# The output projection of an encoder layer as seven block products in one written order

## The chip, the cores and the metric

The kernel is one launch on one core of a Trainium2 chip. The metric is the device time of that launch in microseconds (us); the time of a version is the median of its runs. A profile of one execution is read beside it. In it PE is the matrix engine (TensorE), PEld its loading of stationary operands, DVE is VectorE, ACT ScalarE, POOL GpSimd, and SP the engine whose queue issues most DMAs.

## The reference

One encoder layer is applied to two inputs, 1024 rows ("sample") and 256 rows ("prompt") of width 1024, with the same weights. Two attention branches give `o_a` and `o_b`; a gate merges them, the merged rows go through the output projection, and a squared-ReLU MLP follows.

```python
merged = gates[:, :, 0] * (o_a.reshape(b, S, A_Q) @ w_branch_a) + gates[:, :, 1] * (o_b @ w_branch_b)
x = x + merged @ w_out                      # the output projection: 1280 x 1024 times 1024 x 1024
h = _rmsnorm(x, g_mlp)
return x + jnp.square(jax.nn.relu(h @ w_up)) @ w_down
```

All of it is float32. The kernel keeps that precision by splitting every matmul operand into a high part (a copy rounded to the matrix engine's fast float32 form, on ACT) and a low part (the operand minus the high part, on DVE), and by adding three matmuls, low x high, high x low and high x high, for each product.

## The kernel before

The 1280 rows are 10 tiles of 128 rows (`NT`), tiles 0 to 7 the sample, 8 and 9 the prompt. The stages follow one another on the matrix engine: input projection and attention, the two branch products with their gates, the output projection, then the MLP's up and down products.

**The branch products** are 48 jobs in the list `jobs`. Each makes 128 columns of `merged`, transposed, for one of three row blocks (`BLOCKS`: rows 0-511, 512-1023, 1024-1279) and puts them into the wide tile `mT`. The last 12 jobs are the second half of the `a` columns, block by block. During them `fetch` and `prepare` load and split the projection's weights.

**The output projection** (from L1605) runs in two halves `hh` of 512 output columns. In each, for each row tile `t`, `split_m` splits the tile's eight 128 x 128 pieces of `mT`, `mm3` (L192) makes 24 matmuls 128 x 128 by 128 x 512 (8 pieces, three matmuls each) in one PSUM bank, and DVE adds the bank to the residual tile `x2[t]` (L1653, L1662). In the second half the tile is then normalised: ACT squares it and sums (L1665), ACT takes the root (L1667), DVE the reciprocal (L1672), DVE scales it with `gm` into `xn[t]` (L1673), SP stores `x2[t]`. One tile later PE turns `xn` with eight transposes (`turned`, L336) into two banks of tag `pt`, of which there are two, and ACT copies these out (L1577, L1560).

**The MLP's up product** is already made of seven block products in place of eight (the scheme of Strassen and Winograd). Its left operands are the four quarters of the normalised sample rows and three sums of them, `S1`, `S2`, `S3` (and later `S4`), made on DVE by `combine` (L1587, L1589, L1592), first for 3/4 of the columns, then for the last quarter. `halves` splits them (L310 high part on ACT, L312 low part on DVE). The product on the quarter `A11` comes first, then `A12`, `S2`, `S3`, `S1`, `A22`. A product is `seven` (L345): 12 matmuls. `right_pair` makes the matching sums of the weights (L391) and splits them.

**What sets the order.** Until the projection's second half, a planner orders each engine's instructions and gives out buffers. From `tc.manual_schedule` on, which stands at the start of the second half, each engine executes its instructions in the order in which the code writes them: an instruction that waits holds up all that follow on its engine. So the places of `next(turning)`, `next(more)`, `part(t + 2)` and `steps_of(sums, ..)` in the loop over `t` are the queue orders of ACT and DVE. The buffers are 33 slots of 4 KB per partition with tag `m` (`slot`), 10 of tag `w` (`wslot`), 6 in the pool `late` (tag `l4`), and eight PSUM banks: `mm` 3, `sc` 2, `pt` 2, `pv` 1.

Of the kernel before, what the change touches and what calls it, by code (L numbers as in the profile page):

```python
# [10 lines left out]
F32 = mybir.dt.float32  # L11
# [4 lines left out]
P = 128  # L16
D = 1024
# [80 lines left out]
def encoder_kernel(  # L98
# [8 lines left out]
    def x_rows(t):  # L107
        return x_sample[0, P * t : P * (t + 1), :] if t < 8 else x_prompt[0, P * (t - 8) : P * (t - 7), :]
# [18 lines left out]
    def slot(name, shape=(P, D), dt=F32):  # L127
        return slots.tile(list(shape), dt, name=name, tag="m", bufs=N_M)
# [4 lines left out]
    def qslot(name, shape, dt=F32):  # L133
        return narrows[0].tile(list(shape), dt, name=name, tag="q", bufs=N_Q)
# [49 lines left out]
    def split(hi, lo, src):  # L184
        nc.scalar.activation(hi, src, AF.Copy)  # L185
        nc.vector.tensor_tensor(lo, src, hi.bitcast(F32), op=ALU.subtract)  # L186
# [25 lines left out]
    n_out = len(specs)  # L212
    for h in range(2):
        for i in range(4):
            specs.append((w_out3[:, 2 * i : 2 * i + 2, 512 * h : 512 * h + 512], (P, 2, 512), wslot))
    specs[n_out + 2] = specs[n_out + 2][:2] + (slot,)
# [92 lines left out]
    def split_steps(hi, lo, src):  # L309
        nc.scalar.activation(hi, src, AF.Copy)  # L310
        yield
        nc.vector.tensor_tensor(lo, src, hi.bitcast(F32), op=ALU.subtract)  # L312
        yield
# [54 lines left out]
    def right_pair(cols, out, make=wslot, vector=False, step=KC):  # L368
# [13 lines left out]
        def part(src, shape):  # L382
            out.append((wslot("whi", shape, F32R), wslot("wlo", shape, F32R)))
            yield from split_steps(*out[-1], src)
# [973 lines left out]
    def split_m(t, hh, out):  # L1358

        n = 2 if hh else KC  # L1360
        mhi = [qslot("mhi", (P, n, P), F32R) if hh else slot("mhi", (P, n, P), F32R) for _ in range(KC // n)]
        mlo = slot("mlo", (P, KC, P), F32R)
        for c in range(0, KC, 2):
            split(mhi[c // n][:, c % n : c % n + 2, :], mlo[:, c : c + 2, :], mT.at(c, P * t, P, 2))
            yield
        out += [(mhi[k // n][:, k % n, :], mlo[:, k, :]) for k in range(KC)]

    first_m = []
    early_m = split_m(0, 0, first_m)
    if True:  # L1370
# [100 lines left out]
        sgs = {}  # L1471

# [38 lines left out]
        for i, (x, b, c) in enumerate(jobs):  # L1511
# [7 lines left out]
            if i in (1, 4, 22, 26):  # L1519
                fetch()  # L1520
            elif i in (5, 8, 33, 35):
                w_as[(5, 8, 33, 35).index(i)] = weight(0)
            elif i in (38, 40, 42, 44):
                prepare()
# [14 lines left out]
            if i > len(jobs) - 6:  # L1539
                next(early_m, None)  # L1540

    att_pool.close()


    x2 = [slot(f"x2_{t}") for t in range(NT)]
    for t in range(NT):
        nc.sync.dma_start(x2[t], x_rows(t))
# [60 lines left out]
    with ExitStack() as pre:  # L1608
        late = pre.enter_context(tc.tile_pool(name="late", bufs=4))

        def lslot(name, shape=(P, D), dt=F32):
            return late.tile(list(shape), dt, name=name, tag="l4", bufs=6)

        for i in (4, 5, 6):
            specs[n_out + i] = specs[n_out + i][:2] + (lslot,)
        gm = slot("gm2")
        nc.sync.dma_start(gm, g_mlp[0].partition_broadcast(P))
        xn = {}
        p0 = []
        b0 = right_up(0, p0, slot)  # L1620

        def ahead():

            yield from b0
            yield from halves(A11, raws_h[0, 0])
            yield from halves(A12, raws_h[0, 1])

        more, sums = ahead(), combine()
        for hh in range(2):
            sl = slice(512 * hh, 512 * hh + 512)  # L1630
            ws = [weight(0) for _ in range(4)]
            parts = {}
            if hh:

                ctx.enter_context(tc.manual_schedule(engines=ALL))

            def part(t):
                if t < NT:
                    parts[t] = []
                    run(split_m(t, hh, parts[t]))  # L1640

            if hh:
                part(0)
            else:
                parts[0] = first_m
            part(1)
            for t in range(NT):
                m = parts.pop(t)
                ps = bank("mm")
                run(mm3(ps, [(m[k], (ws[k // 2][0][:, k % 2, :], ws[k // 2][1][:, k % 2, :]))  # L1650
                             for k in range(KC)]))
                if hh == 0:
                    nc.vector.tensor_tensor(x2[t][:, sl], x2[t][:, sl], ps, op=ALU.add)  # L1653
                    part(t + 2)
                    if 2 <= t < 6:
                        prepare()
                    elif t in (6, 7):
                        next(more)
                    continue
                turning = (turn_sample if t < 9 else turn_prompt)(t - 1) if t else iter(())  # L1660
                next(turning, None)
                nc.vector.tensor_tensor(x2[t][:, sl], x2[t][:, sl], ps, op=ALU.add)  # L1662
                xn[t] = slot("xn", (P, D))
                ss = small.tile([P, 1], F32, name="ss")
                nc.scalar.activation(xn[t], x2[t], AF.Square, accum_out=ss)  # L1665
                sd = small.tile([P, 1], F32, name="sd")
                nc.scalar.activation(sd, ss, AF.Sqrt, bias=eps, scale=1.0 / D)  # L1667
                if 0 < t < 7:
                    next(more)
                steps_of(sums, (0, 1, 4)[max(t - 7, 0)])  # L1670
                rs = small.tile([P, 1], F32, name="rs")
                nc.vector.reciprocal(rs, sd)  # L1672
                nc.vector.scalar_tensor_tensor(xn[t], x2[t], rs, gm, op0=ALU.mult, op1=ALU.mult)  # L1673
                nc.sync.dma_start(scr_x[t], x2[t])
                next(turning, None)
                part(t + 2)
                steps_of(more, (1, 1, 1, 1, 1, 3, 2, 0, 0, 0)[t])
                steps_of(sums, (2, 3)[t - 7] if 6 < t < 9 else 0)
        run(sums)
        run(halves(S2, combined[S2]))  # L1680
    narrow.close()
# [6 lines left out]
    C11, C12, C21, C22 = range(4)  # L1688

# [206 lines left out]
    with ExitStack() as pre:  # L1896
# [30 lines left out]
        def up(j, b, parts, hooks):  # L1927
# [7 lines left out]
            start = begin(parts)  # L1935
# [107 lines left out]
```

## Time and profile before

| | us |
|---|---|
| median of 3 runs | 1674.67 |
| lowest and highest run | 1673.53, 1675.32 |
| the profiled execution, first to last instruction (its span) | 1672.7 |
| first matmul of the output projection | 769.2 |
| its last matmul's start | 885.0 |
| matmuls of the output projection | 480 |

The profile's own time for the execution is its span; what lies before the first and after the last instruction is not in it. The median of the runs is 1.97 us above the span. The page gives the busy time of each engine, the span in 40 slices, the chain of work that ended last (followed back from the last instruction through what released each step), and groups of instructions with count and mean duration. The trace answers for any stretch: the instructions of one engine in order of time, the same chain in detail, or busy time by stretch.

### The profile page before, as it was taken

The page shows a single profiled execution, that of the slowest core. Times are in us where ns is not written, and L with a number is a line of the kernel's source. Part 1 is how long each engine was busy: PE and PEld are TensorE (multiplying, and loading weights), DVE is VectorE, ACT ScalarE, POOL GpSimd, SP SyncE. Part 2 cuts the span into 40 slices and gives each one's busy share as a digit, 9 for nine tenths or more (in the row PEclk, how much of TensorE's full clock was granted, in tenths as well). Part 3 has the DMA queues.
Part 4 walks back from the last instruction along what each step waited for, and adds up shares of the span by engine and source line. Part 5 has one row for each costly group of instructions (what it writes and reads, how often), then busy time and mean ns, then how long its engine had stood idle before and what let it go on. Part 6 is the DMA issues. An engine that isn't in the chain of part 4 may idle for free.

```text
span 1672.7 us, 24767 instructions
## 1 busy us (share of the span) xinstructions
PE 1661.8 (99%) x9256; PEld 1413.9 (85%) x9256; DVE 951.1 (57%) x1534; ACT 714.3 (43%) x1473; POOL 494.3 (30%) x372
## 2 busy tenths in 40 slices
PE   9999999999999999999999999999999999999998
PEld 7898888888888888888888888888888888888886
DVE  6732233455654565667278545445456775867665
ACT  6232323345654655654176333333334333333435
POOL 1212222111112352100100656455554250514240
PEclk9999999999999999999999999999999999999999
DMA  7416552666667794845121443343356934733333
GB/s 256 150 54 126 134 132 75 165 196 189 198 184 228 192 236 134 284 135 193 38 89 59 161 160 120 121 161 125 116 191 230 362 113 137 253 104 107 120 120 126
DMA packets 224176, 262.45 MB, mean 157 GB/s; under 512 B 29486, under 2 KB 153694, under 8 KB 224056
## 3 DMA queue, kind: packets, MB, share of 16 engines
q1 hardware_dynamic: 217000, 242.69, 45.4%
q0 software_dynamic: 6720, 17.65, 5.1%
q8 instruction: 73, 1.20, 0.3%
q10 hardware_dynamic: 336, 0.53, 0.1%
q14 instruction: 47, 0.39, 0.1%
HBM read 175.13 MB, written 90.92 MB: 159 GB/s over the span
## 4 chain that ended last, share of the span: by engine, by line
PE 96%; ACT 2%; DVE 1%; DMA 1%; issue 0%; SPq 0%; DVEq 0%; ACTq 0%
PE dn L345 22%; PE x L345 19%; PE mm L192 14%; PE z L345 10%; PE v L819 6%; PE y L345 5%; PE mm L345 5%; PE pv L345 3%; PE sc L345 3%; PE pt L1193 2%; PE pv L1209 2%; PE sc L553 1%; PE pv L600 1%; PE pt L586 1%; PE tr L336 1%; PE sc L1167 1%
## 5 line engine op out<-in xcount | busy, mean ns | idle before, releaser
L345 PE MATMUL dn<-dhi,ulo 128*128 128x512 f32 x448 | 174.3, 389 | 0.0
L345 PE MATMUL dn<-dlo,uhi 128*128 128x512 f32 x448 | 174.3, 389 | 0.0
L345 PE MATMUL dn<-dhi,uhi 128*128 128x512 f32 x448 | 174.3, 389 | 0.0
L345 PE MATMUL x<-chi,wlo 128*128 128x512 f32 x424 | 166.5, 393 | 0.0
L345 PE MATMUL x<-clo,whi 128*128 128x512 f32 x424 | 165.6, 390 | 0.0
L345 PE MATMUL x<-chi,whi 128*128 128x512 f32 x424 | 165.0, 389 | 0.0
L312 DVE TENSOR_TENSOR wlo<-ta,whi 128x1024 fp32r<-128x1024 f32 x30 | 56.3, 1876 | 174.0 <-ACT whi L310 174.0
L312 DVE TENSOR_TENSOR wlo<-raw,whi 128x1024 fp32r<-128x1024 f32 x60 | 89.6, 1494 | 103.1 <-ACT whi L310 98.2
L391 POOL TENSOR_TENSOR tb<-raw 128x512 f32<-128x512 f32 x25 | 32.3, 1290 | 363.7 <-DMA raw<-in_w_in_dram 111.8
L345 PEld LDWEIGHTS dn<-dhi,ulo 128*128 128x128 f32 x448 | 84.1, 188 | 17.6
L345 PEld LDWEIGHTS dn<-dhi,uhi 128*128 128x128 f32 x448 | 84.1, 188 | 17.4
L345 PEld LDWEIGHTS dn<-dlo,uhi 128*128 128x128 f32 x448 | 84.1, 188 | 17.4
L345 PEld LDWEIGHTS x<-chi,whi 128*128 128x128 f32 x424 | 79.6, 188 | 17.1
L345 PEld LDWEIGHTS x<-chi,wlo 128*128 128x128 f32 x424 | 79.8, 188 | 15.1
L345 PEld LDWEIGHTS x<-clo,whi 128*128 128x128 f32 x424 | 79.8, 188 | 14.6
L1735 POOL TENSOR_TENSOR t<-raw,t 128x1024 f32<-128x1024 f32 x16 | 46.4, 2924 | 149.2 <-DMA raw<-in_w_down_dram 149.2
L186 DVE TENSOR_TENSOR ulo<-uraw,uhi 128x1024 fp32r<-128x1024 f32 x56 | 86.1, 1558 | 4.4 <-ACT uhi L185 4.4
L1886 DVE TENSOR_TENSOR v<-v,dn 128x512 f32<-128x512 f32 x90 | 59.7, 683 | 42.3 <-PE dn L345 42.3
L186 DVE TENSOR_TENSOR dlo<-raw,dhi 128x1024 fp32r<-128x1024 f32 x32 | 50.1, 1590 | 46.3 <-ACT dhi L185 45.3
L1986 POOL TENSOR_TENSOR u<-u,u 128x640 f32<-128x640 f32 x16 | 25.1, 1569 | 173.3 <-ACT u L1904 173.3
L345 PE MATMUL dn<-dhi,up 128*128 128x512 f32 x224 | 73.5, 389 | 0.0
L345 PE MATMUL z<-chi,wlo 128*128 128x512 f32 x184 | 71.6, 389 | 0.0
(319 smaller groups left out, 4619.2 us busy)
## 6 DMA issues: line engine op xcount, KB each, us to landing
scr_u<-u SPq DMA_DIRECT2D x112, 320.0 KB, 2.6
uraw<-scr_u SPq DMA_DIRECT2D x56, 512.0 KB, 3.9
raw<-in_w_down_dram SPq DMA_DIRECT2D x36, 512.0 KB, 6.7
raw<-in_w_up_dram SPq DMA_DIRECT2D x32, 512.0 KB, 5.2
raw<-in_w_in_dram SPq DMA_DIRECT2D x25, 512.0 KB, 5.2
sg<-scr_g SPq DMA_DIRECT2D x32, 256.0 KB, 6.2
uraw<-scr_u SPq DMA_DIRECT2D x28, 256.0 KB, 4.5
qk<-scr_kb SPq DMA_DIRECT2D x48, 128.0 KB, 2.6
```

The source lines that it names most:

```text
L186: nc.vector.tensor_tensor(lo, src, hi.bitcast(F32), op=ALU.subtract)
L192: nc.tensor.matmul(ps, a, b, start=i == 0, stop=i == len(seq) - 1)
L312: nc.vector.tensor_tensor(lo, src, hi.bitcast(F32), op=ALU.subtract)
L336: nc.tensor.transpose(ps[:, P * i : P * (i + 1)], xn[t][:, P * k : P * (k + 1)], ident)
L345: nc.tensor.matmul(ps, a, b, start=first and i == 0, stop=last and i == len(seq) - 1, skip_group_check=True)
L391: (nc.vector if vector else nc.gpsimd).tensor_tensor(o, x, y, op=ALU.subtract)
L819: nc.tensor.matmul(ps[:, :n], a, b, start=k == 0 and j == 0, stop=k == KC - 1 and j == 2)
L1193: nc.tensor.transpose(ps[:, P * k : P * k + P], s[:, h, P * b : P * b + P], ident)
L1209: nc.tensor.matmul(pv[HALVES[h], P * i : P * i + P], src, pt[:, at + 2 * b + h, :], start=b == 0, stop=b == W // P - 1, skip_group_check=True)
L1735: nc.gpsimd.tensor_tensor(o, a, b, op=ALU.subtract)
L1886: nc.vector.tensor_tensor(v, v, ps, op=ALU.add)
L1986: nc.gpsimd.tensor_tensor(u[S1], u21, u22, op=ALU.add)
```

## The change

The projection's left operand (1024 sample rows and 256 prompt rows, seen as two halves of 640 rows) and `w_out` are cut into four blocks each, and seven products of 640 x 512 by 512 x 512 take the place of eight. Each product `n` has five steps `t` (four tiles of 128 rows of the sample half and one of the prompt), a step being `six`: 12 matmuls 128 x 128 by 128 x 512. Results that several blocks of the output share stay in their PSUM bank: products 1 and 2 are joined in one bank, and so are 3, 4, 5 and 6, and after each product DVE adds what the bank holds then to the residual (`total`), 35 additions of 128 x 512 in place of 20.

The sums of the left operands (`sum1` to `sum4`) and of the weight blocks (`differ`) are on GpSimd. So are the low parts of the weights of products 5 and 6 and of the up product's first weights (`low`). The blocks of `w_out` are loaded eight times in all, 1 MB each, in two DMAs. The manual order begins before the first product. The rows of the first half are finished in product 4 and normalised there, those of the second half in product 6; a row's `scale` comes one step after its `norm`, and its transposes two steps after. The sums for the up product start in the last step (34), after the copies of tile 6. Tile 7 is turned, and the rest of the sums made and `S2` split, in the middle of the up product's first block (`entered`).

```diff
-    def split(hi, lo, src):
+    def split(hi, lo, src, low=None):
         nc.scalar.activation(hi, src, AF.Copy)
-        nc.vector.tensor_tensor(lo, src, hi.bitcast(F32), op=ALU.subtract)
+        (low or nc.vector).tensor_tensor(lo, src, hi.bitcast(F32), op=ALU.subtract)
...
+        ORDER = (A12, S1, S4, A11, S2, S3, A22)
+        TO = (C11, C22, C12, C11, C12, C22, C21)
+        TAGS = (("mm", "mm", "mm", "sc", "sc"), ("pt", "pt", "pv", "sc", "sc"), None, ("mm", "mm", "mm", "sc", "sc"),
+                None, None, None)
...
+        def differ(self, o, a, b):
+            for x, y, z in zip(self.b[o], self.b[a], self.b[b]):
+                nc.gpsimd.tensor_tensor(x, y, z, op=ALU.subtract)
...
+        def right(self, n, name, low=None):
+            out = self.rights[n] = []
+            for src in self.b[name]:
+                hi, lo = wslot("whi", (P, 2, 512), F32R), wslot("wlo", (P, 2, 512), F32R)
+                split(hi, lo, src, low)
...
+        def left(self, n, i):
...
+            split(hi, lo, self.source(n, i))
...
+        def sum1(self, i):
...
+            nc.gpsimd.tensor_tensor(self.s1[i], self.quarter(1, 0, i), self.quarter(1, 1, i), op=ALU.add)
...
+        def product(self, n, t):
...
+            six(self.banks[t], self.rights[n], lefts, n in (0, 1, 3), n in (0, 2, 6))
+
+        def total(self, n, t):
+            c = self.TO[n]
+            v = x2[self.row(c, t)][:, 512 * (c % 2) : 512 * (c % 2) + 512]
+            nc.vector.tensor_tensor(v, v, self.banks[t], op=ALU.add)
+
+        def ahead(self, n):
+
+            if n == 0:
+                self.right(1, "t")
+                self.block("b22", 1, 1)
+                self.rows(1)
+                yield
+                for i in range(3):
+                    self.left(1, i)
+                    self.sum2(i)
+                    yield
+                for i in range(3):
+                    self.sum4(i)
...
+            elif n == 2:
+                self.right(3, "b11")
+                self.block("b22", 1, 1)
+                yield
+                for i in range(3):
+                    self.left(3, i)
+                    self.sum3(i)
+                    yield
...
+            elif n == 4:
+                self.right(5, "b22", nc.gpsimd)
+                self.block("b21", 1, 0)
+                yield
+                for i in range(3):
+                    self.left(5, i)
+                    yield
+                self.differ("b21", "b21", "t")
+            elif n == 5:
+                self.right(6, "b21", nc.gpsimd)
+                yield
+                for i in range(3):
+                    self.left(6, i)
+                    yield
...
     def right_up(j, out, make=wslot):
-        return right_pair([w_up3[:, :, c : c + P] for c in (2 * P * j, 2 * P * j + P)], out, make, j == 1)
...
+        return right_pair([w_up3[:, :, c : c + P] for c in (2 * P * j, 2 * P * j + P)], out, make, j == 1,
+                          low=None if j else nc.gpsimd)
...
+    for n in range(7):
+        side = out.ahead(n)
...
+        for t in range(5):
+            step = 5 * n + t
+            out.product(n, t)
+            turning = iter(())
+            if turns and turns[0][0] <= step:
+                r = turns.pop(0)[1]
+                turning = (turn_sample if r < 8 else turn_prompt)(r)
+            next(turning, None)
+            out.total(n, t)
+            if scales:
+                scale(scales.pop())
+            if n in (4, 6):
+                r = out.row(0 if n == 4 else 2, t)
+                scales.append(r)
+                turns.append((step + 2, r))
+                norm(r)
+            next(turning, None)
+            next(side, None)
+            if step == 28:
+                steps_of(b0, 2)
+            if 29 <= step <= 32:
+                steps_of(lefts, 2)
+            if step in (30, 31, 33):
+                steps_of(b0, 2)
+            if step == 34:
+                steps_of(sums, 6)
+    scale(scales.pop())
+    run(b0)
+    pre.close()
+
+    def entered():
+        run(turn_sample(7))
         run(sums)
         run(halves(S2, combined[S2]))
...
-        def begin(parts):
+        def begin(parts, mid=None):
 
             x, y = bank("mm", "x"), bank("pt", "y")
-            seven(x, A11, parts[0], 0, last=False)
+            seven(x, A11, parts[0], 0, last=False, mid=mid)
```

In the code after the change, `norm` is the squaring and the root on ACT, `scale` the reciprocal and the scaling on DVE with the store, and `lefts` splits the quarters `A11` and `A12` for the up product, half a quarter at a time. Of `b0` (the up product's first weights) two steps at step 28 are the loads and the four sums on GpSimd, and each two after that a high part on ACT and a low part on GpSimd.

More of the change, by code (lines that the diff above doesn't have):

```diff
@@ L1605, in right_up @@
     def right_up(j, out, make=wslot):
-        return right_pair([w_up3[:, :, c : c + P] for c in (2 * P * j, 2 * P * j + P)], out, make, j == 1)
[L1608 to L1678, printed above, removed]
@@ new lines, in scale, with first_lefts @@
+    def scale(t):
+        rs = small.tile([P, 1], F32, name="rs")
+        nc.vector.reciprocal(rs, sds.pop(t))
+        nc.vector.scalar_tensor_tensor(xn[t], x2[t], rs, gm, op0=ALU.mult, op1=ALU.mult)
+        nc.sync.dma_start(scr_x[t], x2[t])
+    def first_lefts():
+        yield from halves(A11, raws_h[0, 0])
+        yield from halves(A12, raws_h[0, 1])
+    out.sum1(2)
+    out.left(0, 2)
+    scales, turns, lefts = [], [], first_lefts()
+    for n in range(7):
+        side = out.ahead(n)
+        if n == 3:
+            gm = slot("gm2")
+            nc.sync.dma_start(gm, g_mlp[0].partition_broadcast(P))
+        for t in range(5):
+            step = 5 * n + t
[23 more added lines that the diff above has]
+                steps_of(sums, 6)
```

124 lines of the change are left out of this document (95 added, 29 removed).

## The prediction

> **What bounds the kernel now.** I read the page first: busy time, slices, the chain that ended last.
>
> ```profile
> span 1672.7 us, 24767 instructions
> PE 1661.8 (99%) x9256; PEld 1413.9 (85%) x9256; DVE 951.1 (57%) x1534; ACT 714.3 (43%) x1473; POOL 494.3 (30%) x372
> ...
> PEclk9999999999999999999999999999999999999999
> ...
> PE 96%; ACT 2%; DVE 1%; DMA 1%; issue 0%; SPq 0%; DVEq 0%; ACTq 0%
> ```
>
> The matrix engine is busy throughout at full granted clock, and 96% of the chain is its own work. So a matmul removed is time gained, as long as nothing else becomes late. Next come the instructions of line 192, and the chain in order of time around the projection.
>
> ```profile
> L192 PE MATMUL mm<-whi,mlo x160: 389/389/477, 769.2 to 884.5; 128*128 128x512 f32 x160
> ...
> L192 PE MATMUL mm<-whi,mhi x160: 389/389/397, 769.7 to 885.0; 128*128 128x512 f32 x160
> ```
> ```profile
> by line: PE mm L192 59.3%; PE x L345 9.1%; PE z L345 5.2%; ACT xn L1665 3.2%; PE y L345 3.2%; PE pv L345 3.2%; PE tr L336 2.4%; ACT hraw L1577 1.9%; DVE x L1662 1.7%; PE sc L345 1.6%; ACT mhi L185 1.5%; DVE clo L312 1.4%; ACT chi L310 1.1%;
> ...
> 834.67 0.87 PE tr L336 x8
> 835.54 5.47 PE mm L192 x24
> 841.02 0.87 PE tr L336 x8
> ...
> 871.20 0.96 ACT chi L310
> ...
> 895.78 2.72 PE z L345 x12
> ```
> ```profile
> 889.11 0.50 PE L345 MATMUL y<-chi,wlo 128*128 128x512 f32 x1 [0.15 <-ACT praw L1560]
> ...
> 892.80 0.48 PE L345 MATMUL x<-chi,wlo 128*128 128x512 f32 x1
> ```
>
> Three groups of 160 make the 480 matmuls. One is counted 389 ns, but they are pipelined: twelve take 2.72 (the 895.78 row), 0.2267 each. From one turned tile to the next pass 841.02 - 834.67 = 6.35, so a tile's eight transposes cost 6.35 - 24 x 0.2267 = 0.91. At 889.11 PE waits 0.15, and at 892.80 it starts the up product's block S2. The chain through this stage is not PE alone: it also runs through VectorE's addition (L1662), ScalarE's square, copies and high parts, and VectorE's low part. ScalarE's and VectorE's instructions in order of time show that loop:
>
> ```profile
> 867.41 1.06 ACT L1665 ACTIVATE xn<-x 128x1024 f32<-128x1024 f32 x1 [0.94 <-DVE x L1662]
> ...
> 868.79 1.18 ACT L1577 ACTIVATE hraw<-tr 128x256 f32<-128x256 f32 x4
> 869.85 1.35 ACT L185 ACTIVATE mhi<-mT 128x256 fp32r<-128x256 f32 x4
> 871.07 1.07 ACT L310 ACTIVATE chi<-hraw 128x1024 fp32r<-128x1024 f32 x1
> ```
> ```profile
> 866.69 0.68 DVE L1662 TENSOR_TENSOR x<-x,mm 128x512 f32<-128x512 f32 x1
> ...
> 872.18 1.22 DVE L312 TENSOR_TENSOR clo<-hraw,chi 128x1024 fp32r<-128x1024 f32 x1 [0.43 <-ACT chi L310]
> 873.32 0.68 DVE L1662 TENSOR_TENSOR x<-x,mm 128x512 f32<-128x512 f32 x1
> ...
> 878.29 0.95 DVE L1587 TENSOR_TENSOR s<-hraw 128x768 f32<-128x768 f32 x1
> 879.27 0.96 DVE L1589 TENSOR_TENSOR s<-s,hraw 128x768 f32<-128x768 f32 x1
> ...
> 884.64 1.82 DVE L1592 TENSOR_TENSOR hraw<-hraw 128x768 f32<-128x768 f32 x2
> ...
> 886.98 0.42 DVE L1587 TENSOR_TENSOR s<-hraw 128x256 f32<-128x256 f32 x1
> ...
> 888.61 0.17 DVE L1672 RECIPROCAL rs<-sd 128x1 f32<-128x1 f32 x1
> ...
> 890.01 0.76 DVE L1592 TENSOR_TENSOR hraw<-hraw 128x256 f32<-128x256 f32 x2
> 890.68 2.36 DVE L312 TENSOR_TENSOR clo<-s,chi 128x1024 fp32r<-128x1024 f32 x2
> ```
>
> From an addition to the next, 6.63: addition to square 0.72, square and root 1.38, copies 1.06, the tile's high parts 1.22, a quarter's high part until its low part starts 1.11, low part 1.14. VectorE takes its queue in order, so the addition at 873.32 waited behind that low part. The loop is as long as a tile's 6.35 on PE, so it hides.
>
> **The change, part by part.** *Matmuls.* 480 become 7 x 5 x 12 = 420: 60 x 0.2267 = **13.6 us gained**. The ten turned tiles stay. From the first matmul to S2 pass 892.80 - 769.2 = 123.6 now; PE's own work there will be 35 x 2.72 + 10 x 0.91 + 2 x 2.72 (A11 and A12) = 109.7.
>
> *The loop.* A step is now 2.72, or 3.63 with a turned tile. In products 4 and 6 each step still has addition, square, root, and in six of the ten steps (21 to 23 and 30 to 32) a left part split on the same two engines: 0.72 + 1.38 + 1.11 + 1.14 = 4.35, and 5.41 with copies. Queued behind the waiting low part is the next addition, behind that the next square, and PE waits for the scaled tile and for the two transpose banks.
> Product 4, from the end of its first step: the square ends at 2.10, two high parts of product 5's weights (0.96 each, the 871.20 row) at 4.02, the second square at 5.40, additions follow at 7.65, 13.06 and 17.5, the last copies that free the banks at 20.7, and tile 3 is turned at 21.1. PE alone would be there at 5 x 2.72 + 4 x 0.91 = 17.24: 3.9 lost.
>
> *The end.* From the end of step 30: additions at 4.35, 8.70 and 14.11; then copies of tile 5 until 17.27, a weight's high part 18.23, tile 9's square and root 19.61, copies of tile 6 20.7. Only now start the six sums: 0.98 and 0.9 for two pairs, 1.82 for the last two, 5.5 in all, to 26.3. Tile 9's scaling (888.61 to 890.01) takes 1.40, the six short sums 886.98 to 888.61 and 890.01 to 890.68, 2.30, and the first low part of S2 1.22: 31.2. PE has 4 x 2.72 + 5 x 0.91 + 2 x 2.72 = 20.87 to do meanwhile: 10.3 lost. Before, the sums lay under tiles 7 to 9. After S2, VectorE's low parts for S2 (second), S3 and S1 and one pair of 0.69 come to 6.0 against 5.44 of matmuls: 0.5 more. The 0.15 that PE waits there now goes.
>
> *GpSimd.* From 769 to 893 it now does four small sums from 807 on, nothing else. Whether its new work costs VectorE time, stretches show where both work:
>
> ```profile
> 955.52 2.31 DVE L312 TENSOR_TENSOR wlo<-raw,whi 128x1024 fp32r<-128x1024 f32 x1
> ...
> 1340.66 5.30 DVE L186 TENSOR_TENSOR dlo<-raw,dhi 128x1024 fp32r<-128x1024 f32 x2
> 1345.88 2.35 DVE L186 TENSOR_TENSOR ulo<-uraw,uhi 128x1024 fp32r<-128x1024 f32 x2
> ```
> ```profile
> 955.00 1.75 POOL L391 TENSOR_TENSOR ta<-raw 128x512 f32<-128x512 f32 x1
> 956.70 2.28 POOL L391 TENSOR_TENSOR ta<-raw,tb 128x512 f32<-128x512 f32 x1
> ...
> 1339.12 5.75 POOL L1735 TENSOR_TENSOR t<-raw,t 128x1024 f32<-128x1024 f32 x2 [23.70 <-DMA raw<-in_w_down_dram]
> ```
> ```profile
> 807.10 1.29 POOL L391 TENSOR_TENSOR tb<-raw 128x512 f32<-128x512 f32 x1 [111.41 <-PE mm L192]
> ```
> ```profile
> L1735 POOL TENSOR_TENSOR t<-raw,t x16: 2402/2994/3455, 1339.1 to 1604.6; 128x1024 f32<-128x1024 f32 x16
> ```
>
> Two low parts alone take 2.35, beside two GpSimd sums 5.30. They alternate: at 955.52 the low part waits until GpSimd is done at 956.7, then GpSimd's next (begun 956.70, 2.28 long) waits for it. So an instruction of either that reads two SBUF operands holds something for its whole length: 2.40 for GpSimd's 128x1024, 1.29 for 128x512, and 1.14 for a low part on VectorE. Additions from PSUM read one such operand and are free of it.
> Held from the first product to S2: by GpSimd 20 large (two each in three left sums, six differences of weights, eight low parts) and 8 small, 20 x 2.40 + 8 x 1.29 = 58; by VectorE 26 low parts (eight of weights, twelve of left parts, four of A11 and A12, two of S2), seven of half size (0.6 each, an estimate from the 0.68 row less the overlap that 1.22 against 1.14 shows), ten scalings (1.40 less the reciprocal's 0.17) and the up product's sums, 26 x 1.14 + 7 x 0.6 + 10 x 1.2 + 5.5 + 2.3 = 54. Together **112 against PE's 109.7**, unevenly spread: this is my main reason.
> Its cost lies between nothing (the queues miss each other) and a turn taken at each meeting; by the 5.30 row I take the second. Laid into the orders above: in product 4, GpSimd's two low parts and two differences hold 3.2-5.6, 6.8-9.2, 10.3-12.7 and 13.9-16.3; tile 1's scaling gets its turn only at 12.7 and the second left part at 16.3, and tile 3 is turned at 25.5: 8.3 lost in place of 3.9. At the end, a sum waits once for the low part of the up product's last weight (2.4), and the loops run 0.9 later (a low part and a scaling that wait): 13.6 lost in place of 10.3. In products 1 and 2 GpSimd's sums put VectorE's second left part of product 3 2.6 past its need; that hangs on some twenty turns taken exactly so, and I take half of 2.6, 1.3.
>
> The Trainium skill, Perfetto Trace Analysis, section Optimizing Scalar/DVE Operations, warns that since both share a read port, moving work between these two might not help; by it the eight low parts moved here are a loss, 2.40 against 1.14 of the shared time. The sum has them so already.
>
> *What I cost at nothing.*
>
> ```profile
> raw<-in_w_out_dram SPq DMA_DIRECT2D x8, 512.0 KB, 4.2
> ```
>
> w_out is now loaded in 16 such DMAs. Each block is asked for one product (13.6) before its split; without that cover a product would wait 4.2 and more. On SP's queue stand behind them the residual's ten loads, the first five asked for with the first blocks, 12 jobs ahead of the products, and the stores of the tiles, for which nobody waits here. Removed are the splits of eight weight tiles and of `mT` twice; the new splits are as many or fewer, and only their places count. Of the 35 additions (20 before) those on a path stand in the loops above.
>
> *Sum:* -13.6 + 1.3 + 8.3 + 13.6 + 0.5 - 0.15 = **+10**. Against the execution's span of 1672.7 that is 1682.7; the runs' median is 1.97 above the span, so 1674.67 + 10 = 1684.6.
>
> **Rivals.** (1) *All hidden*: 1674.67 - 13.6 = 1661.1. For it: PE's share; against it: the loop, already as long as its cover. (2) *Only the end waits*: if ScalarE and VectorE keep pace, the sums start at 16.0 after step 30, S2 is ready at 26.4: 5.5 lost, -13.6 + 5.5 + 0.5 - 0.15 = -7.7, **1666.9, faster**. It decides where the left part's low part does not hold the next addition; the 873.32 row speaks against it. (3) *Loops wait but GpSimd costs nothing* (the queues happen to miss each other): -13.6 + 3.9 + 10.3 + 0.5 - 0.15 = +1, 1675.6. Against it the 5.30 row. (4) *A colder PE*: the forecast, and PE slower after its waits at the end, 4.8 for tile 9 and 2.5 for S2 by the order above. The longest wait that I see now is short:
>
> ```profile
> PE warm L727 <- POOL ident masks.py:199: 1.4, 1, 1.4
> ```
>
> and the clock stays full, so no row prices it; twelve matmuls at half pace would be 2.7 more, 1687.3. The Trainium skill, TensorE: Matmul & The Clock Gate, Part 1, has the clock halve after an idle window of about 3.4 us; no run here shows it yet.
>
> **Numbers.** Forecast 0.47 (its own range 1679 to 1690: GpSimd's share of the loss, 9, halved, or the whole 2.6 and some 4 of turns more), rival 1 0.06, rival 2 0.17, rival 3 0.20 (0.03 of it faster, 0.14 the same, 0.03 slower), rival 4 0.10. About 0.2% (3.3 us) is what a measurement of this kernel can tell from no change. Faster by more: 0.06 + 0.17 + 0.03 = 0.26; within: 0.14; slower by more: 0.47 + 0.10 + 0.03 = 0.60. The range 1666 to 1690 leaves out rival 1, part of rivals 2 and 4 and the forecast's tail, under 0.2 together.
>
> **What would show it.** Right: 420 projection matmuls at 0.2267; waits of PE before transposes of tiles 1 to 3 (on VectorE's scaling or ScalarE's copies), and before S2 on VectorE's low part, 10 or more in all; low parts of 2 to 3.5 beside GpSimd. Wrong: no wait at S2 (then the order of sums is not what I read), low parts near 1.22 while GpSimd works, or a late load before a product.

## The result and the profile after

| | before | after |
|---|---|---|
| median of 4 runs each, us | 1674.39 | 1687.96 |
| lowest and highest run | 1673.53, 1675.32 | 1686.74, 1689.11 |
| span of the profiled execution | 1672.7 | 1684.9 |
| first projection matmul to the first matmul of S2 | 123.6 | 132.28 |

After/before is 1.0076, 95% interval 1.006 to 1.0093: slower by 13.6 us, of which the spans of the two profiled executions show 12.2 (the changed kernel's was its fastest of four). The forecast was 1684.6.

The page of the changed kernel: busy times, the clock's line, the shares of the chain.

```profile
span 1684.9 us, 24611 instructions
...
PE 1658.0 (98%) x9196; PEld 1407.7 (84%) x9196; DVE 987.8 (59%) x1488; ACT 712.4 (42%) x1420; POOL 569.7 (34%) x400
...
PEclk9999999999999999999998999999999999999999
...
PE 92%; DVE 3%; ACT 2%; issue 1%; DMA 1%; SPq 0%; DVEq 0%; ACTq 0%
```

The 60 matmuls, worth 13.6 us, are gone (9256 - 9196), yet PE's busy time fell by 3.8 us only, one slice of its clock reads 8, and 4% of the chain left PE. So two things grew: PE's idle time (span less busy) from 10.9 to 26.9 us, and the time of part of its work, which ran at a lower clock behind the longest waits. The idle time is in PE's waits from 765 to 915 us (who waited for whom: total, times, longest):

```profile
PE tr L331 <- DVE xn L1758: 12.2, 3, 5.1
PE tr L331 <- ACT hraw L1710: 1.8, 3, 0.8
PE x L340 <- ACT c L2040: 1.3, 1, 1.3
PE wo L340 <- DVE mlo L186: 0.8, 1, 0.8
```

Before, the same stretch had one wait of 0.2. Now transposes wait for VectorE's scaled tile and for ScalarE's copies out of the two banks, S2 waits once for ScalarE's copy of A11's bank, and product 3 once for a low part. The chain in order of time (start, us, what), first in product 4, then from step 30 on:

```profile
835.34 1.05 ACT mhi L185
...
836.42 2.94 DVE mlo L186
839.36 0.61 DVE x L1442
...
839.99 1.16 ACT xn L1751 x2
...
868.92 0.70 DVE x L1442
...
871.03 1.05 ACT chi L305
...
872.10 1.23 DVE clo L307
873.33 0.60 DVE x L1442
...
874.03 2.60 DVE xn L1758
...
891.05 3.04 DVE s L1722
...
902.45 5.49 PE x L340 x12
```

This is the loop that the prediction named: high part on ScalarE, low part on VectorE, the addition queued behind it, the next square behind that. At the end a scaling takes 2.60 and a sum 3.04, where 1.28 and 0.96 are the times without GpSimd's reads (gpsimd_reads_out, below). The low part of 2.94 stands beside GpSimd's work, in whose rows in order of time no gap is left from 833.20 to 844.87:

```profile
833.20 5.08 POOL L186 TENSOR_TENSOR wlo<-oraw,whi 128x1024 fp32r<-128x1024 f32 x2 [17.63 <-ACT whi L185]
838.24 6.63 POOL L1377 TENSOR_TENSOR oraw<-oraw 128x1024 f32<-128x1024 f32 x2
```

The last row of the chain above is S2: 5.29 from its first matmul to the next product's (the piece's 5.49 counts the last one's tail), where twelve took 2.72 before. PE's rows at the wait ahead of it, and stretches (busy time, then granted clock):

```profile
899.23 1.94 PE L331 MATMUL tr<-ident,xn 128*128 128x128 f32 x8 [4.63 <-DVE xn L1758]
902.45 0.79 PE L340 MATMUL x<-chi,wlo 128*128 128x512 f32 x1 [1.28 <-ACT c L2040]
903.04 0.63 PE L340 MATMUL x<-clo,whi 128*128 128x512 f32 x1
```
```profile
902.45:905.00 2.55, 2.55 (x6) 0.50 0.00 0
...
907.74:910.00 2.26, 2.26 (x11) 0.97 0.03 7
```

The clock is 0.50, and from the second matmul on they start 0.43 apart in place of 0.2267: what rival 4 describes, on top of the forecast's waits. The clock was also low behind two earlier waits (0.80 from 840 to 848.66, 0.68 from 876.78 to 882.06), but the chain has no piece of PE from 828.67 to 853.17 and from 868.90 to 902.45, so of PE's slow work only S2's lies on it.

### The profile page after: what moved, and what is told of

The parts are those of the page before. It is cut to its first block, busy times and chain, and to the rows that moved or that the text cites. A ratio compares the mean times of both kernels' runs of the same rounds, so it can differ in the third digit from the quotient of the medians.

```text
span 1684.9 us, 24611 instructions
## 1 busy us (share of the span) xinstructions
PE 1658.0 (98%) x9196; PEld 1407.7 (84%) x9196; DVE 987.8 (59%) x1488; ACT 712.4 (42%) x1420; POOL 569.7 (34%) x400
## 4 chain that ended last, share of the span: by engine, by line
PE 92%; DVE 3%; ACT 2%; issue 1%; DMA 1%; SPq 0%; DVEq 0%; ACTq 0%
PE dn L340 22%; PE x L340 20%; PE z L340 10%; PE mm L192 8%; PE v L814 6%; PE mm L340 5%; PE y L340 5%; PE sc L340 3%; PE pv L340 3%; PE wo L340 3%; PE pt L1188 2%; PE pv L1204 2%; PE sc L548 1%; PE pv L595 1%; PE pt L581 1%; DVE mlo L186 1%
## 5 line engine op out<-in xcount | busy, mean ns | idle before, releaser
L340 PEld LDWEIGHTS dn<-dhi,uhi 128*128 128x128 f32 x448 | 84.1, 188 | 17.5
L340 PEld LDWEIGHTS dn<-dlo,uhi 128*128 128x128 f32 x448 | 84.1, 188 | 17.5
L340 PEld LDWEIGHTS x<-chi,wlo 128*128 128x128 f32 x424 | 80.3, 189 | 17.1 <-ACT c L2040 1.7
L616 POOL DMA_DIRECT2D scr_b<-o x44 | 23.8, 544 | 152.7 <-DVE o L267 88.7
```

What stands on the lines that cost most here:

```text
L340: nc.tensor.matmul(ps, a, b, start=first and i == 0, stop=last and i == len(seq) - 1, skip_group_check=True)
L616: nc.gpsimd.dma_start(scr_b[g][i][:, qa : qa + nq], o[:, c : c + nq])
```

## The experiments

Measured in each trace are: "product 4", from total(20), the addition after step 20, to the end of tile 3's transposes, taken as 0.91 after their start (17.24 would be PE's own work); "step 30 to S2", from total(30) to S2's first matmul (20.87); "block", from the first projection matmul to the first matmul of the up product's prompt part, which holds all that any edit touches. Where that first matmul stands moves from 768.3 to 775.9 us between executions, ahead of all edits, so stages are measured from it.

| kernel | median us | ratio to before, 95% | product 4 | step 30 to S2 | block |
|---|---|---|---|---|---|
| before | 1674.4 | | | | 142.7 |
| the changed kernel | 1688.0 | 1.0076, 1.006-1.0093 | 25.4 | 33.5 | 154.0 |
| left5_early | 1676.6 | 1.0008, 0.9999-1.0016 | 17.0 | 33.2 | 144.4 |
| first_lefts_early | 1687.4 | 1.0081, 1.0064-1.0099 | 25.4 | 27.8 | 152.2 |
| gpsimd_reads_out | 1679.5 | 1.0029, 1.0019-1.0038 | 22.4 | 30.9 | 146.6 |
| keep_busy | 1684.4 | 1.006, 1.0047-1.0074 | 25.4 | 33.5 | 151.7 |
| lows_on_vector | 1687.5 | 1.0082, 1.0065-1.0098 | 24.6 | 36.2 | 154.8 |
| end_reordered | 1688.7 | 1.0082, 1.0066-1.0097 | 25.4 | 30.4 | 156.8 |
| both | 1680.1 | 1.0033, 1.002-1.0046 | 17.0 | 30.3 | 149.4 |
| both_lefts | 1681.2 | 1.0039, 1.0025-1.0053 | 17.0 | 24.7 | 146.6 |
| both2 | 1676.1 | 1.0008, 0.9999-1.0017 | 17.0 | 30.4 | 144.2 |
| both2_keep | 1676.0 | 1.0009, 1.0-1.0018 | 17.1 | 30.3 | 143.8 |
| both2_b0 | 1674.7 | 1.0, 0.9991-1.0009 | 17.1 | 28.9 | 142.4 |
| fewer_in_30 | 1672.8 | 0.9988, 0.9979-0.9997 | 17.0 | 25.8 | 140.8 |

The medians of before beside the experiments were 1674.9 to 1675.2.

### The loop of product 4: left5_early

```diff
             elif n == 3:
...
                 for i in range(3):
                     self.left(4, i)
+                    if i == 2:
+                        self.left(5, 0)
                     yield
+                self.left(5, 1)
+                self.left(5, 2)
...
             elif n == 4:
...
                 for i in range(3):
-                    self.left(5, i)
                     yield
```

> One part moved: the three splits of product 5's left operand go from product 4 (one a step) into product 3, whose steps have no norm. If product 4 loses its 8.2 us because its loop of addition, square, left part and low part is longer than its 3.63 us of matmuls and transposes (my theory), total(20) to the end of tile 3's transposes falls from 25.4 us to 17.2-18, and the run is 7 to 8 us shorter than the changed kernel, about 1680. If GpSimd's instructions alone hold VectorE there, 17.2 + 4.3 = 21.5 stay and the run is about 4 us shorter (1684). If the waits are due to something else (the two transpose banks, the cold clock), nothing changes (1688).

Product 4 took 17.0: all of its 8.2 us came back, though GpSimd's work there was the same. VectorE in order of time, in the same place as the chain above:

```profile
837.87 0.69 DVE L1442 TENSOR_TENSOR x<-x,wo 128x512 f32<-128x512 f32 x1 [0.72 <-PE wo L340]
...
838.66 1.82 DVE L1761 SCALAR_TENSOR_TENSOR xn<-x,rs,gm 128x1024 f32<-128x1024 f32 x1
```

The additions again wait for PE, and a scaling of 1.82 in place of 1.28 hides. So the loop is the cause and the hold makes it worse. The block is shorter by 9.6: 8.6 from total(20) to total(30) (24.0 + 16.3 before, 16.3 + 15.4 now, so product 5 gains 0.9 of it), 0.3 from there to S2, and some 0.7 of S2's slow matmuls (4.62 against 5.29).

### GpSimd's share: gpsimd_reads_out and lows_on_vector

```diff
-        (low or nc.vector).tensor_tensor(lo, src, hi.bitcast(F32), op=ALU.subtract)
+        if low:
+            low.memset(lo.bitcast(F32), 0.0)
+        else:
+            nc.vector.tensor_tensor(lo, src, hi.bitcast(F32), op=ALU.subtract)
...
-            for x, y, z in zip(self.b[o], self.b[a], self.b[b]):
-                nc.gpsimd.tensor_tensor(x, y, z, op=ALU.subtract)
```

The same is done in `split_steps`, and sums 2 to 4 of the left operand are left out like the differences: the kernel does not compute the layer, and only its times are used.

> Leaves out the differences of the weight blocks and sums 2 to 4 of the left operand, and fills the low parts of the weights of products 5 and 6 and of the up product's first weights with zeros on GpSimd (an instruction that writes and reads nothing) in place of computing them. GpSimd has then almost no two-operand instruction in the stage; all of PE's, VectorE's and ScalarE's work is as it was. If the two engines hold a shared thing when they read two operands (my theory), low parts near GpSimd's work fall to 1.14-1.22, product 4's loss falls from 8.2 to about 4, the end's by about 3: 6.5 to 7.5 us shorter, about 1681. If GpSimd's work costs VectorE nothing (rival 3), the run stays at 1688.

The block is 7.5 shorter, product 4 by 3.0 (5.2 of the 8.2 stay), the end by 2.6. VectorE's rows from product 4, where the loop alone is left:

```profile
835.41 1.23 DVE L189 TENSOR_TENSOR mlo<-mT,mhi 128x1024 fp32r<-128x1024 f32 x1 [2.73 <-ACT mhi L185]
...
837.34 1.28 DVE L1762 SCALAR_TENSOR_TENSOR xn<-x,rs,gm 128x1024 f32<-128x1024 f32 x1
```

1.23 stands where 2.94 stood and 1.28 where 2.58 did: rival 3 falls. GpSimd is idle beside these two rows. Where it writes its zeros and reads nothing, a low part is as short:

```profile
861.94 2.74 POOL L311 MEMSET wlo<- 128x1024 f32 x3
```
```profile
862.83 1.22 DVE L313 TENSOR_TENSOR clo<-hraw,chi 128x1024 fp32r<-128x1024 f32 x1
```

So the hold needs GpSimd to read.

```diff
-                self.right(5, "b22", nc.gpsimd)
+                self.right(5, "b22")
...
-                self.right(6, "b21", nc.gpsimd)
+                self.right(6, "b21")
...
-                          low=None if j else nc.gpsimd)
+                          low=None)
```

> One part undone: the low parts of the weights of products 5 and 6 and of the up product's first weights go back from GpSimd to VectorE. GpSimd holds the shared thing 8 x 2.40 = 19.2 us less, VectorE works 8 x 1.14 = 9.1 us more, partly in its late loops. If the time is lost because two-operand instructions of the two engines exclude each other (my theory), the net is a gain: two of the eight lie in product 4's first step and four in product 6's loop, each worth up to 2.40 - 1.14 = 1.3, so 1 to 5 us shorter than the changed kernel (1683-1687), and VectorE's sums at the end are no longer of 1.5 and 3.0 us but of 0.95. If GpSimd's low parts are free, VectorE's queue grows by 2.3 in product 4 and 4.6 at the end: 3 to 6 us longer (1691-1694).

A miss: 1687.45, neither shorter by 1 nor longer by 3. VectorE's rows of product 6 show why:

```profile
873.74 0.69 DVE L1442 TENSOR_TENSOR x<-x,wo 128x512 f32<-128x512 f32 x1 [0.89 <-PE wo L340]
876.92 1.23 DVE L307 TENSOR_TENSOR clo<-hraw,chi 128x1024 fp32r<-128x1024 f32 x1 [2.49 <-ACT chi L305]
878.07 1.22 DVE L307 TENSOR_TENSOR wlo<-raw,whi 128x1024 fp32r<-128x1024 f32 x1
879.20 0.68 DVE L1442 TENSOR_TENSOR x<-x,wo 128x512 f32<-128x512 f32 x1
...
879.99 1.28 DVE L1758 SCALAR_TENSOR_TENSOR xn<-x,rs,gm 128x1024 f32<-128x1024 f32 x1
```

The scaling is 1.28 again, but the weight's low part now stands in the loop, between the left part's and the addition: from addition to addition 879.20 - 873.74 = 5.46. What was saved in the hold was paid in the queue. The page Perfetto Trace Analysis of the Trainium skill, section Optimizing Scalar/DVE Operations, says that moving work between these two engines might not help; here 1687.5 with these low parts on VectorE against 1688.0 with them on GpSimd agrees with it.

### The clock: keep_busy

```diff
+        def keep(n):
+            ps, w = bank("pv", "keep"), p0[0][0]
+            for i in range(n):
+                nc.tensor.matmul(ps, w[:, 0, :], left(A11, 0)[0], start=i == 0, stop=i == n - 1)
+
...
             run(halves(S3, combined[S3]))
             yield
+            keep(16)
             run(turn_prompt(9, ("pt", "sc")))
```

> Adds 16 matmuls of 128x128 by 128x512 whose result nobody reads, ahead of tile 9's transposes, so that PE is not idle in the 4.6 us before these; nothing else changes. If S2's twelve matmuls take 5.3 us in place of 2.72 because the clock falls after that wait (rival 4's mechanism), they take 2.7 now and the run is 2 to 2.6 us shorter (1685.5). If the slow matmuls have another cause (S2's operands come late one by one), nothing changes or the run is up to 1 us longer.

S2 started as late after total(30) as before, and its twelve matmuls took 2.86 at full clock (a stretch of PE alone: length, busy time, clock):

```profile
902.86:905.72 2.86, 2.86 (x12) 1.00 0.00 0
```

2.4 us are won at S2 by matmuls that compute nothing that is used, so it was the clock that made S2 slow, and PE's idleness that lowered it. The run is 3.6 shorter by medians, the block 2.3.

### The end: splits earlier, or sums in another order

```diff
-            if 29 <= step <= 32:
-                steps_of(lefts, 2)
+            if step in (28, 29):
+                steps_of(lefts, 4)
```

> One part moved: the high and low parts of the up product's first two left quarters (A11, A12), half a quarter in each of steps 29 to 32, now stand whole in steps 28 and 29, before the loop of product 6. If the end's loss comes from the loop of steps 30 to 34 being late (each step 0.7-2.2 us of high and low part longer), the additions after step 30 come earlier, total(30) to S2 falls from 33.5 to 28-30 us, and the run is 4 to 5 us shorter (1683-1684). If the end is set by the sums and S2's low part behind them alone, and by GpSimd, the splits' place counts for little: within 1.5 us of 1688.

Step 30 to S2 fell by 5.7 as expected, but from total(25) to total(30) the time rose from 16.3 to 20.5 us: the four splits in a row put product 6's first steps back. A miss in the sum. The loss moved to an earlier product.

```diff
             if step == 34:
-                steps_of(sums, 6)
-    scale(scales.pop())
+                steps_of(sums, 4)
...
         run(turn_sample(7))
-        run(sums)
+        steps_of(sums, 4)
...
+            run(halves(S1, combined[S1]))
+            yield
+            run(sums)
             run(halves(S3, combined[S3]))
             yield
+            scale(scales.pop())
+            run(halves(A22, combined[A22]))
+            yield
             run(turn_prompt(9, ("pt", "sc")))
-            run(halves(S1, combined[S1]))
-            yield
-            run(halves(A22, combined[A22]))
-            yield
```

With it `combine` makes S3's sums last, and product S1 stands ahead of S3.

> One part moved, at the end alone: VectorE makes the sums for S1 and S2 and S2's low part first; S3's sums (1.82 + 0.76) and tile 9's scaling (1.45) come behind S2's and S1's low parts; tile 9 is turned behind product S3, and product S1 stands ahead of S3. Product 4 is as it was. If S2 waits for VectorE's chain of sums (my step 'The end'), S2 starts 2.4 + 1.4 = 3.8 us earlier after total(30), 29.7 us in place of 33.5, and the run is about 4 us shorter (1684); S2's matmuls stay slow, since PE still waits 3 to 4 us. If S2 waits for ScalarE or the loop alone, less than 1 us.

S2 did start 3.1 us earlier after total(30), and the block became 2.8 longer. The same happened on top of left5_early:

> left5_early and end_reordered together. They act in different stages, so their gains add: 1676.6 - 4 = 1672.5, a little under the kernel before (1674.7). If they share a cause (a loss taken away in product 4 comes back at the end), the run stays near 1676.

PE's two rows with waits in both, and ScalarE's from there:

```profile
889.32 0.79 PE L340 MATMUL x<-chi,wlo 128*128 128x512 f32 x1 [4.66 <-ACT c L2042]
897.92 0.77 PE L340 MATMUL x<-chi,wlo 128*128 128x512 f32 x1 [3.51 <-ACT c L2084]
```
```profile
895.16 2.13 ACT L305 ACTIVATE chi<-hraw 128x1024 fp32r<-128x1024 f32 x2 [4.00 <-DVE hraw L1728]
897.20 0.58 ACT L2084 ACTIVATE c<-x 128x512 f32<-128x512 f32 x1
```

The bank of S2 could have been copied at 894.4, where S2 ended; the copy stood in ScalarE's queue behind S3's high parts, which waited 4.00 for VectorE's sums. My own order made a new wait. both_lefts added the splits of A11 and A12 in steps 26 to 29 to it:

> As both, and the splits of A11 and A12, half a quarter in each of steps 29 to 32, stand three steps earlier, in steps 26 to 29, where no norm runs. first_lefts_early took 5.7 us from the end and gave 4.2 of it back in steps 28 to 30, where four splits stood in a row behind product 4's lateness; with product 4 on time and the splits one a step, most of the 5.7 should stay: 1672.5 - 3 to 5 = 1668-1670. If VectorE's sum of work from step 26 on is the bound and not its place, nothing is gained (1672).

Again S2 came early (24.7 after total(30)) and the time went elsewhere: total(25) to total(30) took 19.7, for VectorE's low parts there met GpSimd's low parts and sums (2.3 to 2.4 in place of 1.2), and the second wait was 4.24. Its profiled execution was its fastest of five, 2.3 below the median, so its block in the table may flatter it. both2 moved only S3's part behind the copy:

```diff
             run(halves(S1, combined[S1]))
             yield
+            yield
             run(sums)
             run(halves(S3, combined[S3]))
-            yield
             scale(scales.pop())
```

> As both (product 5's left operand split in product 3, the end reordered), but S3's sums and split stand behind ScalarE's copy of the bank of A11 and S2 in ScalarE's queue, not ahead of it. In both, S2 started 4.4 us earlier than in left5_early (889.32 against 893.73), and PE then waited 3.5 us for that copy, which stood behind S3's high part, which waited for S3's sums. If that queue order ate the gain, the second wait goes: 1680.1 - 3.5 = 1676.5 at least, and 1672.5 to 1674 where the 4.4 us stay whole (left5_early's 1676.6 less 3 to 4). If what was gained at S2 is owed in any order (VectorE's sums, scaling and low parts of S2, S1, S3 and A22 as a whole are the bound), the run stays between 1676 and 1680.

The second wait fell from 3.51 to 0.78 and the run by 4.0; the queue order is shown. But both2 is no better than left5_early (144.2 against 144.4): S1 directly after S2 waits 0.78 for the copy that S3 had hidden, tile 9's 0.9 of transposes no longer lie in the wait for S2, and S2 stays slow. Filling that wait changes the clock and nothing else:

```diff
             run(halves(S1, combined[S1]))
             yield
+            keep(16)
             yield
```

> As both2, with 16 matmuls whose result nobody reads between the products on A12 and on S2, in PE's wait of some 4.7 us there. By the clock's fall after such a wait (rival 4's mechanism, as keep_busy showed it) S2's twelve matmuls take 2.8 in place of 5.3 us: up to 2.5 us shorter than both2, less what S1's and S3's low parts, which follow at VectorE's pace, take back; about 1.5 shorter. If S2's matmuls were slow for another reason, no change.

S2's matmuls took 3.0 in place of 5.5 and the median fell by 0.1: the next products wait for VectorE's low parts (0.8) and ScalarE's copies (0.4) instead. In this order the other engines are the bound, and S2's half pace had cost almost nothing (0.4 of the block).

### Less held at the end: both2_b0 and fewer_in_30

```diff
-            if step in (30, 31, 33):
+            if 30 <= step <= 33:
                 steps_of(b0, 2)
```

> As both2, and the last two splits of the up product's first weights (GpSimd's low parts) one step earlier each, in steps 32 and 33. In both these two held VectorE's first sums for S2: 1.32 and 3.12 us in place of 0.95 and 0.96. If the shared hold explains that, S2 starts 1.5 to 2.5 us earlier than in both2 and the run is 1 to 2.5 us shorter; if the low parts then hold the scalings of tiles 6 and 7 instead, nothing is gained (within 1 us of both2).

The first two sums for S2 took 2.03 and 0.96 in place of 1.45 and 3.05, S2 came 1.5 earlier after total(30), the block shrank by 1.9. The last run frees the first step of product 6:

```diff
-            if 29 <= step <= 32:
-                steps_of(lefts, 2)
-            if 30 <= step <= 33:
+            if step in (29, 31, 32):
+                steps_of(lefts, 4 if step == 29 else 2)
+            if step in (29, 31, 32, 33):
                 steps_of(b0, 2)
```

> As both2_b0, and product 6's first loop step is freed: the left split of step 30 goes to step 29 (two splits there), and the split of the up product's first weights from step 30 to 29, where ScalarE has 7.6 us idle. In both2_b0 PE waits 2.47 us for tile 4: its scaling began 4.4 us after total(30), behind a low part that waited for ScalarE's square, and took 2.61 us beside GpSimd's low part. If that loop and that hold are the cause, total(30) comes up to 1.6 us later, but the scaling ends some 2.4 us earlier, PE's wait for tile 4 falls under 0.5 us, and the run is 1.5 to 2.5 us shorter: about 1672.5, under the kernel before by 0.15%. If the sum of VectorE's work from there to the up product is the bound, whatever its order, the run stays within 0.7 us of both2_b0 (1674.7).

VectorE's rows around total(30), which is the addition at 861.17:

```profile
857.58 3.66 DVE L307 TENSOR_TENSOR clo<-hraw,chi 128x1024 fp32r<-128x1024 f32 x2
861.17 0.68 DVE L1442 TENSOR_TENSOR x<-x,wo 128x512 f32<-128x512 f32 x1
862.41 0.69 DVE L1442 TENSOR_TENSOR x<-x,wo 128x512 f32<-128x512 f32 x1 [0.57 <-PE wo L340]
...
863.59 1.28 DVE L1761 SCALAR_TENSOR_TENSOR xn<-x,rs,gm 128x1024 f32<-128x1024 f32 x1
```

total(30) is 1.5 later than in left5_early's order (16.9 after total(25), against 15.4), the scaling alone and short, PE's wait for tile 4 gone. 1672.84, ratio 0.9988 (0.9979 to 0.9997): 0.12% under the kernel before, the least of all, but less than the 0.2% that the prediction took as the least that can be told from no change. PE still waits 3.2 for S2 and 3.2 for tiles 5 and 6.

## Why the prediction came out

By its own terms, in us:

| term | predicted | measured | by |
|---|---|---|---|
| 60 matmuls | -13.6 | -13.6 | x9196; the clean stretch of gpsimd_reads_out: twenty steps of products 0 to 3 in 54.43, 2.72 each |
| product 3's start | +1.3 (2.6 by turns) | +0.8 | the wait for `mlo` |
| product 4 | +8.3; 3.9 of it without GpSimd | +8.2; 5.2 | 25.4 - 17.24; 22.4 - 17.24 |
| the end | +13.6; 10.3 without GpSimd | +12.7; 10.0 | 33.5 - 20.87; 30.9 - 20.87 |
| after S2 | +0.5 | 0 | covered by S2's slowness |
| S2's matmuls | 0 (rival 4: +2.7) | +2.6 | 5.29 - 2.72 |
| ahead of the first matmul | 0 | +1.0 | 770.17 - 769.2 |
| S2's old wait | -0.15 | -0.15 | |

Predicted +10, measured by terms +11.6, by spans 12.2, by medians 13.6; 0.6 of the spans stays unassigned, and no trace shows the other 1.4.

**The loops.** That product 4's loop is late because the left part's low part stands ahead of the next addition is shown by left5_early, which took just that out. **GpSimd's share** was 3.0 + 2.6 in the two places against 4.4 + 3.3 as predicted; gpsimd_reads_out shows it. The two causes overlap: in product 4 the loop's removal alone gives back all 8.2, the hold's alone 3.0. Without the loop there is slack in which the hold lies hidden.

That product 4's 8.2 lies so near the predicted 8.3 is in part luck, for its two shares miss in opposite directions: 5.2 in place of 3.9 for the loop alone, 3.0 in place of 4.4 for GpSimd. The first has a cause in the trace. The prediction's loop counts square and root as 1.38 in every step, but the first root is preceded by a table load of 1.28 (its row stands in the last section). In gpsimd_reads_out the additions that the prediction puts at 7.65, 13.06 and 17.5 from the end of the first step stand at 8.87, 14.28 and 18.72: all some 1.2 later. No run moved that load.

At the end the sums for the up product begin 20.6 after total(30) (predicted 20.7). S2's first matmul waits, by its row, for ScalarE's copy of A11's bank, which ends at 902.40, and not for VectorE's low part, which the prediction named and which ends at 902.48. The copy stands in ScalarE's queue behind S2's high parts, and these waited 8.10 for VectorE's sums: the bound that the prediction saw, one instruction further on.

**The term that was left out** is S2's pace: the sum has it at nothing, and rival 4, the colder PE, got 0.10, and it came on top of the forecast. Its price was right (2.7 against 2.6) and the waits it rested on were there, the second at half its length (4.63 and 1.28 for 4.8 and 2.5). The forecast left it out for want of a row. keep_busy settles that the clock was the cause. Two smaller misses follow. A slower S2 covers the 0.5 that VectorE would have cost afterwards (in keep_busy, with S2 at full pace, the following products did wait a little: product S1 was broken by a gap of 0.15 at its second matmul). And at the start `sum1`, placed among the last branch jobs, holds VectorE's addition into `mT`:

```profile
766.51 2.35 DVE L1679 TENSOR_TENSOR mT<-mT,sg 128x256 f32<-128x256 f32 x1
...
769.23 0.42 DVE L1679 TENSOR_TENSOR mT<-mT,sg 128x256 f32<-128x256 f32 x1
```
```profile
766.18 2.40 POOL L1412 TENSOR_TENSOR s1m<-mT,mT 128x1024 f32<-128x1024 f32 x1 [3.04 <-DVE mT L1679]
```

2.35 for an addition that takes 0.42 in the next job. The prediction counted the hold from the first product only. No run here undid `sum1` alone, so the 1.0 is argued, not shown; starts vary by more between executions.

**Rivals.** 1 and 2 fall with product 4's waits. 3 falls with gpsimd_reads_out. How much of the loss was order alone is shown by fewer_in_30: the same products and sums on the same engines, in another order, stand some 15 us under the changed kernel, and 2 us under the one before. So 2 of the 13.6 us of the removed matmuls are had. Of the other 11.6 some 8 lie in PE's waits for VectorE and ScalarE (8.5 in its block, 0.2 before), the rest in PE's slower work behind them. That an order exists which wins these too is not shown.

## What to carry to other kernels

Where the bound engine's step is shortened, a loop on the other engines that was just hidden becomes the bound: work out that loop's length from the queue orders, high part, low part, addition, square, and compare it to the new step before anything is moved. Work taken off a late loop pays in full where it goes to steps with no loop of their own (8.2 us for three splits), and comes back one product earlier where four of them land in a row (first_lefts_early: 5.7 us won at the end, 4.2 lost ahead of it). Before a wait at the end is filled or shortened, look what is queued next on the other engines: end_reordered, both and both_lefts brought S2 some 3 us or more nearer to total(30) and made no run shorter.

## What the runs showed of the hardware

- **The clock falls after short waits and not always.** In the changed kernel the matmuls were at half pace after a wait of 5.09 us (start to start 0.43 from 844.76) and after waits of 4.63 and 1.28 us in a row (S2); in keep_busy they were not after waits of 0.99 and 2.16 us (S2 at clock 1.00); after 2.46 they were in one trace (tile 4 of the changed kernel, 876.78, clock 0.50 from 878 to 880) and not in another (left5_early, 868.36, clock 1.00). In fewer_in_30 the fall came after PE had started again: after a wait of 3.16 us S2's first matmuls start 0.23 to 0.33 apart, the next eight 0.40 to 0.43, until 891.13, a stretch of 3.39 us (clock 0.50):

```profile
886.95 0.50 PE L340 MATMUL x<-chi,wlo 128*128 128x512 f32 x1 [3.16 <-ACT c L2042]
...
887.51 0.41 PE L340 MATMUL x<-chi,whi 128*128 128x512 f32 x1
887.74 0.60 PE L340 MATMUL x<-chi,wlo 128*128 128x512 f32 x1
888.14 0.63 PE L340 MATMUL x<-clo,whi 128*128 128x512 f32 x1
...
891.13 0.42 PE L340 MATMUL x<-chi,whi 128*128 128x512 f32 x1
```

  The Trainium skill, TensorE: Matmul & The Clock Gate, Part 1, has the clock halve after an idle window of about 3.4 us, a window that is free-running and does not start anew with the kernel. The length of this stretch agrees with the window. That waits of 2.46 and 3.16 us, shorter than it, were followed by half pace does not agree with the idle window as the page states it, and here the measurement decides; whether the window's phase makes one wait of 2.46 cost and another not, no run shows.
- **GpSimd is free for VectorE where it only writes.** Beside zeros written in place of low parts, a low part took 1.22 (862.83 in gpsimd_reads_out); beside reads in product 4 of the changed kernel, two took 2.42 and 2.94.
- **A table load sits on the loop.** The first root on ScalarE cost 1.28 us more, at 831.16 in the kernel before and at 830.58 in the changed one. In the kernel before it lay under PE's work; in the changed kernel it stands in product 4's first step. It was not moved in any run.

```profile
830.58 1.28 ACT L1753 ACT_TABLE_LOAD   x1
```
